# A two-block transformer on one core: first mixer rewritten with a column-tiled convolution and TensorE's order by hand

## The chip, the cores and the metric

One core of one Trainium2 chip runs the whole program. The metric is the device time of one execution in microseconds. Before the change it was 1336.69 us, the median of 3 runs (1336.37 to 1338.35).

Words used below: PE is TensorE, PEld its weight loads, DVE is VectorE, ACT is ScalarE, POOL is GpSimd, SP is the engine from whose queue nearly all DMAs are issued.

## What is computed

256 tokens of width 1024 pass through one block of a first model and two blocks of a second, in float32. Only the first block's mixer is touched:

```
h = rms_norm(x, norm1_g); proj = h @ w_in            # 1024 -> q, k, v (512 each), u (1024)
q, k = rope(rms_norm(q)), rope(rms_norm(k))          # 8 heads of 64, per-head norm
attn = softmax(q k^T / 8, causal) v
a, g = split(u + glu_b); c = a * sigmoid(g)
conv = silu(layer_norm(depthwise_causal_conv31(c) + dw_b))   # 512 channels, 31 taps
x = x + concat(attn, conv) @ w_out
...
x = x + (silu(h @ w_gate) * (h @ w_up)) @ w_down
```

The second model's blocks follow: a feed-forward, a mixer and a feed-forward, twice.

## The kernel before

Tokens are two tiles of 128 (t = 0, 1). Every large product keeps float32 accuracy with three fp32r matmuls of 512 columns: activations and weights are each split into a hi part (ACT copies to fp32r) and a lo part (DVE subtracts), and `mm3` (L270) adds hi*hi, hi*lo and lo*hi in PSUM. Weights are stored as a list of blocks (`plan`, L80) of 128 x 2048 floats, 1 MB each; `load` (L211) issues one DMA per block on SP into three rotating buffers with the tag raw, `split` (L225) makes hi and lo halves of 1024 columns in eight rotating buffers (wh, wl), and `take` (L257) hands blocks to the matmuls and keeps the splits two blocks ahead. A projection (`project`, L467) is two blocks: 48 matmuls for both tiles.

The tile framework's scheduler orders the instructions of each engine by priority; every engine then runs its own list strictly in order, and SP issues its DMAs strictly in order.

The first mixer (`mixer1`, L672) projects a and g (`project2`, L476: tile 0 for both, then tile 1, since tile 1's input arrives later), adds bias, takes the sigmoid, multiplies, transposes the product into four tiles hc of 128 channels x 286 positions (30 zeros ahead), and convolves. The 31 taps of channels 0 to 127 and 128 to 255, and 12 of the third group, are 74 operations on DVE of 128x256 (`conv_dve`, L733), placed in portions between the other work by `bg` (L746). The other 50 taps are fp32 matmuls on PE with a diagonal 128x128 weight each (`conv_pe`, L714), whose diagonals come by DMA, four at a time (tag dg). Queries and keys are normed per head with eight squares each on ACT (L762), rotated on DVE (`rope`, L523) and transposed (`to_T`, L537). Scores, softmax and transposed probabilities follow (`scores`, L602), the v projection, the attention sum (`attend`, L618: two heads side by side in column tiles of 64), the layer norm of the convolution (L792 to L811), and `w_out` (L491), first its attention half, then its convolution half. `ends` (L450) adds to the residual xres and makes the next block's transposed input (`norm_in`, L299).

At the start (`run`, L970) SP loads an identity, x in two pieces for tile 0, constants, the first weight block in four pieces, x for tile 1 and more blocks; `norm_in` transposes x on PE before the first matmul.

Of the kernel before, what the change touches and what calls it, by code (L numbers as in the profile page):

```python
# [14 lines left out]
P = 128  # L15
# [64 lines left out]
def plan():  # L80
# [3 lines left out]
    b += out_blocks("w_out", (0,), (0, 1))  # L84
# [40 lines left out]
C_DWW = 76  # L125
C_SUB = 200
NCOL = 201
# [48 lines left out]
class K:  # L176
    def __init__(self, tc, aps, pools):
        self.tc, self.nc = tc, tc.nc
        self.w, self.x_in, self.cols_in, self.rows_in, self.sh_in, self.rev_in, self.dg_in, self.out = aps
# [31 lines left out]
    def load(self):  # L211
# [7 lines left out]
        q = n // 4 if i == 0 else n // 2 if i == 1 else n  # L219
        for a in range(0, n, q):  # L220
            self.nc.sync.dma_start(r[:, a : a + q], src[:, a : a + q])
# [3 lines left out]
    def split(self):  # L225
# [9 lines left out]
        for a in range(0, n, h):  # L235
            wh = self.hl.tile([P, 2048 // NPART], F32R, tag="wh", name=self.nm("wh"))
            wl = self.hl.tile([P, 2048 // NPART], F32R, tag="wl", name=self.nm("wl"))
            step = min(h, FIRST_SPLIT if i < 2 else SPLIT)
# [60 lines left out]
    def norm_in(self, t, idx):  # L299

        nc = self.nc
        xh = self.xp.tile([P, D], F32R, tag=f"xh{t}", name=self.nm("xh"))
        xl = self.xp.tile([P, D], F32R, tag=f"xl{t}", name=self.nm("xl"))
# [12 lines left out]
        self.xT[t] = (xh, xl)  # L316

    def xlhs(self, t):
        xh, xl = self.xT[t]
# [155 lines left out]

    def project2(self, widths, between=None):  # L476
# [14 lines left out]
    def w_out(self, lhs0, lhs1, post, nxt, mid=None):  # L491

        ps = [[self.mmt(), self.mmt()] for _ in range(2)]
        for h in range(2):
            (b,) = self.take(1)
            for t in range(2):
                self.block_mm(ps[t][h], b, lambda k: lhs0(t, k), 0, True, False)
        bs = self.take(2, 2)
# [50 lines left out]
    def softmax_rows(self, t, qT, kT, heads, mask):  # L549
# [8 lines left out]
        for g in range(0, n, 2 * per):  # L558
# [7 lines left out]
            for h in hs:  # L566
# [7 lines left out]
                es[h] = s  # L574
        return es, sm
# [25 lines left out]

    def scores(self, qT, kT, mask):  # L602

        out = []
        for t in range(2):
            es, sm = self.softmax_rows(t, qT, kT, list(range(8)), mask[t] if isinstance(mask, list) else mask)
            pt = self.probs_T(t, es, list(range(8)))
            rs = self.small(8, "rs")
            self.nc.vector.reciprocal(rs, sm)

            rb, rr = self.slot(), self.slot()
            self.nc.vector.tensor_copy(
                rb[:, :].rearrange("p (h d) -> p h d", d=64), rs[:, :].unsqueeze(2).broadcast_to([P, 8, 64]))
            self.nc.scalar.activation(rr, self.transpose4(rb), AF.Copy)
            out.append((pt, rr))
        return out

    def attend(self, sc, v):  # L618

        nc = self.nc  # L620
        res = []
        for t in range(2):
            pt, rr = sc[t]
            o = self.att()
            for h in range(8):
                r, c = (h % 2) * 64, (h // 2) * P
                for kb in range(t + 1):
                    nc.tensor.matmul(  # L628
                        o[r : r + 64, c : c + P], v[kb][:, h * 64 : (h + 1) * 64], pt[(h, kb)],
                        start=(kb == 0), stop=(kb == t), tile_position=(0, r))  # L630
            on = self.slot()
            nc.vector.tensor_tensor(on, o, rr, op=ALU.mult)
            res.append(self.split_T(on))
        return res
# [37 lines left out]
    def mixer1(self, nxt):  # L672
# [20 lines left out]

        pa, pg = self.project2((512, 512), between=lambda: self.norm_in(1, 0))
        for t in range(2):
            self.norm_rstd(t)
        hc = [self.slot() for _ in range(4)]
        for c in range(4):
            nc.gpsimd.memset(hc[c][:, 0:30], 0.0)
        for t in range(2):  # L700
            r = self.rstd[t][:, 0:1]
            a, g = self.slot(), self.slot()
            nc.vector.scalar_tensor_tensor(a, pa[t], r, glu[:, :512], op0=ALU.mult, op1=ALU.add)
            nc.vector.scalar_tensor_tensor(g, pg[t], r, glu[:, 512:], op0=ALU.mult, op1=ALU.add)
            nc.scalar.activation(g, g, AF.Sigmoid)
            nc.vector.tensor_tensor(a, a, g, op=ALU.mult)
            tp = self.transpose4(a)
# [3 lines left out]
        w = lambda c, k: self.cols[:, C_DWW + c * 31 + k : C_DWW + c * 31 + k + 1]  # L711
        cps = {}

        def conv_pe(c):  # L714
            ks = list(range(CONV_DVE[c], 31))
            if not ks:
                return
            if not cps:
                cps["bank"] = self.mmt()
            ps = cps[c] = cps["bank"][:, (c % 2) * 256 : (c % 2 + 1) * 256]  # L720
            for g in range(0, len(ks), 4):
                dg = self.sl.tile([P, 512], F32, tag="dg", name=self.nm("dg"), bufs=DG_BUFS)
                nk = len(ks[g : g + 4])
                nc.sync.dma_start(
                    dg[:, : nk * P].rearrange("p (k m) -> p k m", k=nk),
                    self.dg_in[c, ks[g] : ks[g] + nk].rearrange("k p m -> p k m"))
# [340 lines left out]
```

## Time and profile before

| | |
|---|---|
| median of the runs | 1336.69 us |
| the profiled execution, its own time | 1337.39 us |
| its span, first to last instruction | 1335.6 us |
| PE busy | 1308.6 us, 98% |
| DVE busy | 794.9 us, 60% |
| ACT busy | 682.7 us, 51% |
| start of the third projection | 36.06 us |
| first matmul of the first feed-forward | 142.08 us |

Times in the rows count from the span's start. A timeline row merges neighbours of one kind: its second number is the time from the first one's start to the last one's end, and matmuls overlap, so that the spacing of starts, not the length, is what one costs. A plain fp32 matmul leaves two records.

### The profile page before, as it was taken

What the parts mean: (1) busy time and instruction counts of PE and PEld (TensorE: products, weight loads), DVE (VectorE), ACT (ScalarE), POOL (GpSimd) and SP (SyncE); (2) the same over time, 40 slices, a digit from 0 to 9 for tenths busy, and PEclk for the clock granted to TensorE, in tenths of its full rate; (3) what the DMA queues carried; (4) which work ended last, traced back from release to release, by engine and by line L of the source; (5) the groups of instructions that cost most, each with busy time, mean ns of one, the idle gap of its engine ahead of it and who ended that gap; (6) DMA issues with size and microseconds to landing.
All of it is one profiled execution on the core that took longest, in us unless ns stands there. A gap on an engine that the chain in (4) does not pass through costs nothing.

```text
span 1335.6 us, 16190 instructions
## 1 busy us (share of the span) xinstructions
PE 1308.6 (98%) x6226; PEld 1065.8 (80%) x6226; DVE 794.9 (60%) x1249; ACT 682.7 (51%) x1131; POOL 33.4 (3%) x47
## 2 busy tenths in 40 slices
PE   7989999999999999999999999999999999999998
PEld 5767888888888888777888888888888777888886
DVE  5888655545555547897665544755546554755543
ACT  5663644435545435756654444654435856744431
POOL 0100000000000000000000000000000000000000
PEclk9999999999999999999999999999999999999999
DMA  8652465554655554533365555555554452465540
GB/s 297 218 193 85 163 211 189 189 175 157 219 178 189 185 177 157 193 127 115 126 246 191 172 181 183 207 187 189 189 189 170 161 188 99 172 219 185 187 164 32
DMA packets 43470, 235.55 MB, mean 176 GB/s; under 512 B 4864, under 2 KB 13696, under 8 KB 16640
## 3 DMA queue, kind: packets, MB, share of 16 engines
q1 hardware_dynamic: 43392, 234.51, 50.7%
q8 instruction: 49, 0.80, 0.2%
q14 instruction: 29, 0.24, 0.1%
HBM read 233.44 MB, written 1.05 MB: 176 GB/s over the span
## 4 chain that ended last, share of the span: by engine, by line
PE 90%; DVE 4%; ACT 2%; DMA 1%; POOL 1%; issue 1%; SPq 0%; POOLq 0%; DVEq 0%; ACTq 0%
PE mm L272 27%; PE mm L274 27%; PE mm L273 27%; PE tp L382 2%; PE at L565 1%; DVE wl L243 1%; PE tp L308 1%; DMA dg<-dg 1%; PE mm L729 1%; PE tp L520 1%; PE tp L586 1%; PE at L628 1%; DVE slot L741 1%; DMA raw<-w 1%; POOL qf L285 1%
## 5 line engine op out<-in xcount | busy, mean ns | idle before, releaser
L243 DVE TENSOR_TENSOR wl<-raw,wh 128x1024 fp32r<-128x1024 f32 (+2 forms) x430 | 514.3, 1208 | 409.5 <-ACT wh L242 396.4
L242 ACT ACTIVATE wh<-raw 128x1024 fp32r<-128x1024 f32 (+2 forms) x430 | 444.0, 1049 | 500.9 <-PE mm L274 472.9
L272 PE MATMUL mm<-wh,xh 128*128 128x512 f32 (+1 forms) x1168 | 458.5, 393 | 2.5 <-ACT wh L242 2.5
L273 PE MATMUL mm<-wl,xh 128*128 128x512 f32 (+1 forms) x1168 | 456.2, 391 | 0.6 <-DVE wl L243 0.6
L274 PE MATMUL mm<-wh,xl 128*128 128x512 f32 (+1 forms) x1168 | 456.5, 391 | 0.0
L272 PEld LDWEIGHTS mm<-wh,xh 128*128 128x128 f32 x1168 | 219.9, 188 | 48.4 <-ACT wh L242 3.8
L273 PEld LDWEIGHTS mm<-wl,xh 128*128 128x128 f32 x1168 | 219.7, 188 | 46.6 <-DVE wl L243 2.4
L274 PEld LDWEIGHTS mm<-wh,xl 128*128 128x128 f32 x1168 | 219.9, 188 | 44.5 <-issue 0.2
L272 PE MATMUL mm<-wh,slot 128*128 128x512 f32 x536 | 211.0, 394 | 0.0
L274 PE MATMUL mm<-wh,slot 128*128 128x512 f32 x536 | 209.8, 392 | 0.0
L273 PE MATMUL mm<-wl,slot 128*128 128x512 f32 x536 | 209.7, 391 | 0.0
L272 PEld LDWEIGHTS mm<-wh,slot 128*128 128x128 f32 x536 | 100.7, 188 | 21.5 <-issue 1.5
L274 PEld LDWEIGHTS mm<-wh,slot 128*128 128x128 f32 x536 | 100.6, 188 | 20.7
L273 PEld LDWEIGHTS mm<-wl,slot 128*128 128x128 f32 x536 | 100.7, 188 | 20.0
L313 ACT ACTIVATE xh<-tp,cols 128x128 fp32r<-128x128 f32 x128 | 42.5, 369 | 30.4 <-PE tp L308 16.6
L424 DVE SCALAR_TENSOR_TENSOR slot<-mm,rstd,slot 128x512 f32<-128x512 f32 (+1 forms) x60 | 41.7, 702 | 18.3 <-PE mm L274 18.3
L314 DVE SCALAR_TENSOR_TENSOR xl<-tp,cols,xh 128x128 fp32r<-128x128 f32 x128 | 40.6, 346 | 20.0 <-ACT xh L313 19.0
L572 ACT ACTIVATE e<-e,mx 128x128 f32<-128x128 f32 (+1 forms) x80 | 35.4, 446 | 7.6 <-DVE mx L569 7.6
L423 ACT ACTIVATE slot<-mm,rstd 128x512 f32<-128x512 f32 (+1 forms) x60 | 36.5, 658 | 3.6 <-PE mm L274 3.4
L385 DVE TENSOR_TENSOR slot<-tp,slot 128x512 fp32r<-128x512 f32 (+1 forms) x60 | 35.9, 639 | 0.0
L337 ACT ACTIVATE junk<-mm 128x512 bf16<-128x512 f32 x24 | 14.4, 600 | 36.6 <-PE mm L274 36.6
L741 DVE SCALAR_TENSOR_TENSOR slot<-slot,cols,slot 128x256 f32<-128x256 f32 x71 | 32.2, 479 | 0.5
(117 smaller groups left out, 652.8 us busy)
## 6 DMA issues: line engine op xcount, KB each, us to landing
raw<-w SPq DMA_DIRECT2D x209, 1024.0 KB, 4.9
gb<-rows SPq DMA_DIRECT2D x7, 512.0 KB, 5.5
dg<-dg SPq DMA_DIRECT2D x11, 256.0 KB, 2.9
bias<-rev SPq DMA_DIRECT2D x2, 1024.0 KB, 7.4
raw<-w SPq DMA_DIRECT2D x2, 592.0 KB, 3.8
raw<-w SPq DMA_DIRECT2D x4, 256.0 KB, 6.1
raw<-w SPq DMA_DIRECT2D x2, 512.0 KB, 8.4
out<-xres SPq DMA_DIRECT2D x4, 256.0 KB, 2.0
```

Of the source, the lines that this page charges most:

```text
L242: self.nc.scalar.activation(wh[:, o], r[:, i_], AF.Copy)
L243: self.nc.vector.tensor_tensor(wl[:, o], r[:, i_], wh[:, o].bitcast(F32), op=ALU.subtract)
L272: mm(ps, xh, wh, start=start, stop=False)
L273: mm(ps, xh, wl, start=False, stop=False)
L274: mm(ps, xl, wh, start=False, stop=stop)
L313: nc.scalar.activation(xh[:, c], tp[:, j * P : (j + 1) * P], AF.Copy, scale=g)
L314: nc.vector.scalar_tensor_tensor(xl[:, c], tp[:, j * P : (j + 1) * P], g, xh[:, c].bitcast(F32), op0=ALU.mult, op1=ALU.subtract)
L385: nc.vector.tensor_tensor(hlo[:, :cw], tp, hh[:, :cw].bitcast(F32), op=ALU.subtract)
L423: nc.scalar.activation(sg[:, :cw], pg[t], AF.Silu, scale=r)
L424: nc.vector.scalar_tensor_tensor(sg[:, :cw], pu[t], r, sg[:, :cw], op0=ALU.mult, op1=ALU.mult)
L572: nc.scalar.activation(s[:, :nk], s[:, :nk], AF.Exp, bias=mx[:, h : h + 1], scale=-1.0, accum_out=sm[:, h : h + 1])
L741: nc.vector.scalar_tensor_tensor(a, hc[c][:, k : k + 256], w(c, k), a, op0=ALU.mult, op1=ALU.add)
```

## The change

What it does, part by part:

- **Start.** Eight matmuls of zeros stand first on PE. x (transposed on the host) and the first two weight blocks come packed together in four pieces (`first`), the first of them in two DMAs; no transposes on PE for the first input. All eight k-slices are split straight from these pieces (`start`).
- **Order.** Inside `mixer1_body` PE runs in the order in which the code is written (`manual_schedule`); other engines are still scheduled. Transposes and small matmuls stand at chosen places between the projections' matmuls (`project_with`, `w_out`'s `between`).
- **Convolution.** All on PE. For each of four channel groups, four 32-channel quarters are column tiles of 32; a matmul's 128 rows are 32 channels times four shifts of the input by 8, so that 8 matmuls per quarter cover the 32 taps (the last is zero). The shifted input xc is made by 16 DMAs per group from hc, 64 in all, issued as soon as hc is whole (`conv_load`); the weights cw come in two DMAs of 1 MB into raw buffers.
- **Norm of q and k.** One square of 512 columns on ACT and a reduction on DVE, in place of eight squares with accumulated sums.
- **w_out** takes the convolution's half first; its end, with the next block's transposes, lies in the hand-written order too.
- Small tiles elsewhere change their tags; behind the first feed-forward block the order of every engine is as before.

```diff
-FIRST_SPLIT = 512
-DG_BUFS = 2
-CONV_DVE = (31, 31, 12, 0)
-BG = (10, 10, 24, 20)
+XC_BUFS = 3
+WARM = 8
+CG = 8
+CW = CG + 255
...
-    b += out_blocks("w_out", (0,), (0, 1))
+    b += out_blocks("w_out", (0,), (1, 0))
...
+    def start(self):
+        nc = self.nc
+        nc.scalar.dma_start(self.cols[:, C_G : C_G + 8], self.cols_in[:, C_G : C_G + 8])
+        self.x_halves(0)
+        xh, xl = [a[:, :].rearrange("p (t c) -> p t c", t=2) for a in self.xT]
+        parts = []
+        for p in range(4):
+            r = (self.raw if p < 3 else self.gp).tile(
+                [P, 2048], F32, tag="raw" if p < 3 else "bias", name=self.nm("first"))
+            for a, n in ((0, 768), (768, 768)) if p == 0 else ((0, 1536),):
+                nc.sync.dma_start(r[:, a : a + n], self.first_in[p][:, a : a + n])
...
+                nc.scalar.activation(wh[:, o], u, AF.Copy)
+                nc.scalar.activation(xh[:, :, c], x, AF.Copy, scale=g)
+                nc.vector.tensor_tensor(wl[:, o], u, wh[:, o].bitcast(F32), op=ALU.subtract)
...
+    def project_with(self, between, ncols=512, nb=2):
+        ps = [self.mmt(ncols), self.mmt(ncols)]
+        n = 0
+        for i in range(nb):
+            (b,) = self.take(1)
+            nk = b[1][3]
+            for k in range(nk):
+                if n in between:
+                    between[n]()
+                for t in range(2):
+                    self.mm3(
+                        ps[t], *self.xlhs(t)(b[1][2] + k), *self.part(b, k * ncols, ncols),
+                        i == 0 and k == 0, i == nb - 1 and k == nk - 1)
+                n += 1
+        return ps
...
-        pa, pg = self.project2((512, 512), between=lambda: self.norm_in(1, 0))
         for t in range(2):
             self.norm_rstd(t)
+        with self.tc.manual_schedule(engines={PE}):
+            self.mixer1_body(glu, tabs, nxt)
...
+        def glu_T(t):
+            tp = self.transpose4(ag[t])
+            for c in range(4):
+                nc.scalar.activation(hc[c][:, 30 + t * P : 30 + (t + 1) * P], tp[:, c * P : (c + 1) * P], AF.Copy)
+            if t == 1:
+                conv_load()
...
+        def conv_load():
+            for c in range(4):
...
+                for s in range(4):
+                    for i in range(4):
+                        nc.sync.dma_start(
+                            xc[32 * s : 32 * s + 32, i * CW : (i + 1) * CW],
+                            hc[c][32 * i : 32 * i + 32, 8 * s : 8 * s + CW])
...
+        def conv(c):
+            if c % 2 == 0:
+                cps["w"] = self.raw.tile([P, 2048], F32, tag="raw", name=self.nm("cw"))
+                nc.sync.dma_start(cps["w"], self.cw_in[c // 2])
+                cps["bank"] = self.mmt()
...
+            for g in range(CG):
+                for i in range(4):
+                    o = ((c % 2) * 4 + i) * 32 * CG + g * 32
+                    nc.tensor.matmul(
+                        ps[32 * i : 32 * i + 32, :], wt[:, o : o + 32], xc[:, i * CW + g : i * CW + g + 256],
+                        start=(g == 0), stop=(g == CG - 1), tile_position=(0, 32 * i))
...
-                for h in range(8):
-                    c = slice(h * 64, (h + 1) * 64)
-                    nc.scalar.activation(sq[:, c], ps[t][:, c], AF.Square, accum_out=ss[:, h : h + 1])
+                nc.scalar.activation(sq, ps[t], AF.Square)
+                nc.vector.tensor_reduce(ss, sq[:, :].rearrange("p (h d) -> p h d", d=64), axis=AX.X, op=ALU.add)
...
+        pq = self.project_with({3: lambda: glu_T(0), 5: lambda: glu_T(1)})
+        qT, kT = [self.slot(), self.slot()], [self.slot(), self.slot()]
+        q = qk_norm(pq, 0)
+        pk = self.project_with({5: lambda: self.to_T(q[0], qT, 0), 7: lambda: self.to_T(q[1], qT, 1)})
+        k = qk_norm(pk, 1)
+        conv(0)
+        conv(1)
+        self.to_T(k[0], kT, 0)
...
+        st[0][0]()
+        conv(2)
+        self.to_T(k[1], kT, 1)
+        st[1][0]()
+        conv(3)
+        pt = [self.probs_T(0, sm[0][0], heads), {}]
+        st[1][1]()
...
+        pv = self.project_with({
+            1: lambda: ln_a(0), 3: lambda: (probs(heads[:4]), inv(0)), 4: lambda: ln_a(1),
+            6: lambda: (probs(heads[4:]), inv(1)), 7: lambda: ln_b(0)})
+        v = self.vcopy(pv)
+        ln_b(1)
...
+        self.w_out(part(cv, 4), part(att, 0), None, nxt, {
+            2: lambda: att.append(self.attend_t(0, (pt[0], rr[0]), v)),
+            3: lambda: att.append(self.attend_t(1, (pt[1], rr[1]), v))})
...
+        for _ in range(WARM):
+            nc.tensor.matmul(ps[:, :P], z[:, :P], z[:, :P], start=True, stop=True)
+        self.start()
+        self.load()
```

`st` holds the three groups of scores and softmax (tile 0; tile 1, heads 0 to 3 and 4 to 7). In the lists below xc is the shifted input, slot_340 to slot_343 are hc, cw is the convolution's weight.

SP's queue behind the loads of the k and v projections, before the change (raw is a weight block, dg four diagonals):

```order
L221 DMA raw_222<-w 128x2048
L724 DMA dg_942<-dg 128x4x128
L221 DMA raw_395<-w 128x2048
L724 DMA dg_948<-dg 128x4x128
L221 DMA raw_413<-w 128x2048
L221 DMA raw_447<-w 128x2048
L221 DMA raw_559<-w 128x2048
L354 DMA gb_2722<-rows 128x1024
L943 DMA bias_8262<-rev 128x8x256
L221 DMA raw_593<-w 128x2048
L221 DMA raw_869<-w 128x2048
L221 DMA raw_903<-w 128x2048
```

and with it:

```order
L220 DMA raw_366<-w 128x2048
L220 DMA raw_409<-w 128x2048
L802 DMA xc_434<-slot_340 32x263 x16
L802 DMA xc_451<-slot_341 32x263 x16
L802 DMA xc_468<-slot_342 32x263 x16
L802 DMA xc_485<-slot_343 32x263 x16
L220 DMA raw_564<-w 128x2048
L220 DMA raw_598<-w 128x2048
L810 DMA cw_684<-cw 128x2048
L810 DMA cw_798<-cw 128x2048
L220 DMA raw_938<-w 128x2048
```

The 64 copies now stand together, ahead of the two next weight blocks and of cw; before, single loads of diagonals stood between the blocks.

PE between the k projection and the scores, with the change (mm_686 is the convolution's bank, slot_658 is k of tile 0, at the scores):

```order
L271 MATMUL mm_563<-wh_415,xh_102 128x512
L272 MATMUL mm_563<-wl_416,xh_102 128x512
L273 MATMUL mm_563<-wh_415,xl_103 128x512
L816 MATMUL mm_686<-xc_434,cw_684 32x256 x32
L816 MATMUL mm_686<-xc_451,cw_684 32x256 x32
L575 MATMUL tp_753<-sh,slot_658 128x128 x4
L621 MATMUL at_764<-slot_522,slot_520 128x128
```

Before, tap matmuls stood in fours and less between transposes and scores, behind the v projection:

```order
L729 MATMUL mm_941<-slot_344,dg_942 128x256 x4
L520 MATMUL tp_686<-sh,slot_679 128x128 x4
L586 MATMUL tp_729<-sh,e_705 128x128
L729 MATMUL mm_941<-slot_344,dg_948 128x256
L586 MATMUL tp_729<-sh,e_708 128x128
L586 MATMUL tp_729<-sh,e_711 128x128
L565 MATMUL at_756<-slot_627,slot_481 128x256
L565 MATMUL at_757<-slot_627,slot_481 128x256
L586 MATMUL tp_729<-sh,e_714 128x128
```

Two groups of convolution, 32 matmuls each, now stand in one piece ahead of k's transposes, the scores and the v projection.

DVE at the gate, before (L703 and L704 add the bias, L706 multiplies, L243 is a lo split):

```order
L243 TENSOR_TENSOR wl_398<-raw_177,wh_397 128x1024
L704 SCALAR_TENSOR_TENSOR slot_350<-mm_224,rstd_332,gb_132 128x512
L703 SCALAR_TENSOR_TENSOR slot_364<-mm_277,rstd_339,gb_132 128x512
L243 TENSOR_TENSOR wl_402<-raw_177,wh_401 128x1024
L706 TENSOR_TENSOR slot_349<-slot_349,slot_350 128x512
L704 SCALAR_TENSOR_TENSOR slot_365<-mm_302,rstd_339,gb_132 128x512
L243 TENSOR_TENSOR wl_406<-raw_187,wh_405 128x1024
L706 TENSOR_TENSOR slot_364<-slot_364,slot_365 128x512
```

and with the change (L778 and L780 for L704 and L706, L242 for L243; wl_275 is the first lo half of the third projection):

```order
L778 SCALAR_TENSOR_TENSOR slot_356<-mm_271,rstd_192,gb_161 128x512
L780 TENSOR_TENSOR slot_266<-slot_266,slot_352 128x512
L780 TENSOR_TENSOR slot_268<-slot_268,slot_356 128x512
L242 TENSOR_TENSOR wl_275<-raw_198,wh_274 128x1024
L242 TENSOR_TENSOR wl_279<-raw_198,wh_278 128x1024
L242 TENSOR_TENSOR wl_309<-raw_232,wh_308 128x1024
L242 TENSOR_TENSOR wl_313<-raw_232,wh_312 128x1024
```

The first lo half of the third projection stood ahead of the gate, and now stands behind the whole of it.

## Rows read from the trace of the kernel before

**Rows 1.** The page: engines' busy time (1) and the chain that ended last, by engine (4).

```profile
PE 1308.6 (98%) x6226; PEld 1065.8 (80%) x6226; DVE 794.9 (60%) x1249; ACT 682.7 (51%) x1131; POOL 33.4 (3%) x47
...
PE 90%; DVE 4%; ACT 2%; DMA 1%; POOL 1%; issue 1%; SPq 0%; POOLq 0%; DVEq 0%; ACTq 0%
```

**Rows 2.** Table of windows, whole core: stretch, length, busy time of each engine, clock, DMA.

```profile
0.00:8.33 8.33, 2.20 (x9) 1.44 (x9) 0.88 (x4) 2.70 (x5) 0.30 (x5) 1.00 0.62 176
8.33:36.06 27.73, 26.20 (x105) 19.84 (x106) 20.34 (x44) 19.54 (x35) 1.35 (x6) 1.00 0.83 306
36.06:142.08 106.02, 97.11 (x506) 76.70 (x504) 88.38 (x196) 58.92 (x174) 8.86 (x8) 1.00 0.49 164
142.08:1335.60 1193.52, 1183.13 (x5611) 967.81 (x5609) 685.31 (x1007) 601.54 (x920) 22.92 (x28) 1.00 0.50 174
```

**Rows 3.** Timeline of PE: first matmuls, four transposes, steady matmuls; start, length, line, form, count.

```profile
8.33 0.80 PE L272 MATMUL mm<-wh,xh 128*128 128x512 f32 x1 [1.59 <-ACT wh L242]
...
13.00 0.43 PE L272 MATMUL mm<-wh,xh 128*128 128x512 f32 x1
...
39.03 0.60 PE L520 MATMUL tp<-sh,slot 128*128 128x128 f32 x4
...
150.06 0.39 PE L272 MATMUL mm<-wh,xh 128*128 128x512 f32 x1
...
158.90 0.39 PE L272 MATMUL mm<-wh,xh 128*128 128x512 f32 x1
```

**Rows 4.** Timeline of PE: scores (L565), old convolution (L729), attention in two column tiles (L628).

```profile
72.82 1.16 PE L565 MATMUL at<-slot,slot 64*128 64x128 f32 x16
...
85.20 1.14 PE L565 MATMUL at<-slot,slot 64*128 64x256 f32 x8
...
95.49 3.80 PE L729 MATMUL mm<-slot,dg 128*128 128x256 f32 x16 [1.63 <-DMA dg<-dg]
99.22 1.96 PE L628 MATMUL at<-slot,slot 128*64 128x128 f32 x28
```

**Rows 5.** DVE's groups by line and form, 0 to 142 us: busy us, mean ns.

```profile
L243 DVE TENSOR_TENSOR wl<-raw,wh 128x1024 fp32r<-128x1024 f32 x30 | 36.2, 1219 | 2.8 <-ACT wh L242 2.1 <-DMA slot<-rows 0.6
L741 DVE SCALAR_TENSOR_TENSOR slot<-slot,cols,slot 128x256 f32<-128x256 f32 x71 | 32.2, 479 | 0.5
...
L533 DVE TENSOR_TENSOR slot<-mm,slot 128x256 f32<-128x256 f32 x4 | 1.7, 418 | 0.0
...
L704 DVE SCALAR_TENSOR_TENSOR slot<-mm,rstd,gb 128x512 f32<-128x512 f32 x2 | 1.5, 751 | 3.5 <-PE mm L274 3.5
...
L706 DVE TENSOR_TENSOR slot<-slot,slot 128x512 f32<-128x512 f32 x2 | 1.4, 685 | 0.0
```

**Rows 6.** The same, ACT.

```profile
L242 ACT ACTIVATE wh<-raw 128x1024 fp32r<-128x1024 f32 x31 | 32.0, 1071 | 11.6 <-DMA raw<-w 7.1 <-PE mm L274 4.5
...
L808 ACT ACTIVATE slot<-tp,cols 128x128 f32<-128x128 f32 x8 | 3.0, 454 | 0.0
...
L709 ACT ACTIVATE slot<-tp 128x128 f32<-128x128 f32 x8 | 1.6, 294 | 0.0
...
L808 ACT ACT_TABLE_LOAD x1 | 1.3, 1283 | 0.0
L705 ACT ACTIVATE slot<-slot 128x512 f32<-128x512 f32 x2 | 1.3, 632 | 3.9 <-DVE slot L704 3.9
```

**Rows 7.** Timeline of SP: start, length and count of DMA issues.

```profile
2.58 1.86 SPq L221 DMA_DIRECT2D raw<-w  x4
...
9.11 0.33 SPq L354 DMA_DIRECT2D gb<-rows  x1
...
35.81 0.43 SPq L724 DMA_DIRECT2D dg<-dg  x1
```

**Rows 8.** DMA, 0 to 150 us: GB/s by slices of 3.75 us; issue to landing, us.

```profile
GB/s 123 220 341 427 337 152 433 304 310 55 321 354 374 302 214 151 133 85 194 33 247 70 256 85 292 272 283 27 144 78 117 0 0 55 225 203 81 0 210 227
...
raw<-w SPq DMA_DIRECT2D x19, 1024.0 KB, 5.0
```

More of the change, by code (lines that the diff above doesn't have):

```diff
@@ L557, in softmax_rows, with group @@
         sm = self.small(8, "sm")
-        for g in range(0, n, 2 * per):
+        def group(g):
             hs = heads[g : g + 2 * per]
@@ L574, in softmax_rows @@
                 es[h] = s
+        if parts is not None:
+            parts += [lambda g=g: group(g) for g in range(0, n, 2 * per)]
+        else:
+            for g in range(0, n, 2 * per):
+                group(g)
         return es, sm
@@ L607, in scores, with attend_t @@
             pt = self.probs_T(t, es, list(range(8)))
[L608 to L615, printed above, removed]
-        return out
-    def attend(self, sc, v):
[L620 to L624, printed above, removed]
-            for h in range(8):
[L626 to L634, printed above, removed]
+            out.append((pt, self.inv_rows(sm)))
+        return out
+    def attend_t(self, t, sc, v):
+        nc = self.nc
+        pt, rr = sc
+        o = self.att()
+        for h in range(8):
+            r, c = (h % 2) * 64, (h // 2) * P
+            for kb in range(t + 1):
+                nc.tensor.matmul(
+                    o[r : r + 64, c : c + P], v[kb][:, h * 64 : (h + 1) * 64], pt[(h, kb)],
+                    start=(kb == 0), stop=(kb == t), tile_position=(0, r))
+        on = self.slot()
+        nc.vector.tensor_tensor(on, o, rr, op=ALU.mult)
+        return self.split_T(on)
+    def attend(self, sc, v):
+        return [self.attend_t(t, sc[t], v) for t in range(2)]
     def scaled_tables(self, t, co, si, w, mul):
@@ L692, in mixer1, with mixer1_body @@
             tabs.append(a)
-        pa, pg = self.project2((512, 512), between=lambda: self.norm_in(1, 0))
         for t in range(2):
             self.norm_rstd(t)
+        with self.tc.manual_schedule(engines={PE}):
+            self.mixer1_body(glu, tabs, nxt)
+    def mixer1_body(self, glu, tabs, nxt):
+        nc = self.nc
+        pa = self.project()
+        ag = []
+        for t in range(2):
+            a = self.slot()
+            nc.vector.scalar_tensor_tensor(a, pa[t], self.rstd[t][:, 0:1], glu[:, :512], op0=ALU.mult, op1=ALU.add)
+            ag.append(a)
+        pg = self.project()
         hc = [self.slot() for _ in range(4)]
@@ L712, in mixer1 @@
         cps = {}
[L714 to L718, printed above, removed]
-                cps["bank"] = self.mmt()
[L720 to L726, printed above, removed]
-                for j, k in enumerate(ks[g : g + 4]):
-                    d = dg[:, j * P : (j + 1) * P]
-                    nc.tensor.matmul(ps, d, hc[c][:, k : k + 256], start=(k == ks[0]), stop=(k == 30))
@@ L744, in mixer1 @@
-        it = conv_dve()
-        def bg(n):
-            for _ in range(n):
-                next(it, None)
-        ops = []
-        for which in range(2):
-            bg(BG[which])
-            ps = self.project()
-            dst = [self.slot(), self.slot()]
+        acc = [self.slot()[:, :256] for _ in range(4)]
+        def conv_load():
+            for c in range(4):
+                if c == 0:
+                    xc = self.gp.tile([P, 2048], F32, tag="bias", name=self.nm("xc"))
+                else:
+                    xc = self.gp.tile([P, 4 * CW], F32, tag="xc", name=self.nm("xc"), bufs=XC_BUFS)
+                for s in range(4):
[3 more added lines that the diff above has]
+                            hc[c][32 * i : 32 * i + 32, 8 * s : 8 * s + CW])
+                xcs.append(xc)
@@ L756, in mixer1, with qk_norm @@
+        def qk_norm(ps, which):
+            res = []
             for t in range(2):
@@ L1020, in build @@
         ):
-            K(tc, (w, x, cols, rows, sh, rev, dg, out), (cp, raw, hl, sl0, xp, gp, sm, psm, pst)).run()
+            K(tc, (w, x, first, cols, rows, sh, rev, cw, out), (cp, raw, hl, sl0, xp, gp, sm, psm, pst)).run()
 def kernel(**inputs):
```

167 lines of the change are left out of this document (93 added, 74 removed).

## The prediction

> **What bounds the kernel now.** I read the page first: TensorE is busy 98% of the span and the chain that ended last runs through it for 90% [rows 1]. So only what TensorE has to do, or waits for, counts. The table of windows then says where the change can act [rows 2]: it touches the time up to 142.08 us, where the feed-forward's first matmul starts; the order of every engine behind that is the same in both programs, and there PE is busy 1183.1 of 1193.5 us. In the first 142.08 us it is busy 125.5. The rest is 16.6 us of idle time, and 22.8 us of the busy time is the convolution, so a rewritten mixer has something to win. Time is the profiled execution's (1337.4 us, span 1335.6); the median of the runs is 0.7 below it.
>
> Prices used throughout. A 512-column matmul takes 0.227 us (39 starts in 8.84 us) [rows 3]. A transpose takes 0.1 us: four take 0.60 us, of which the last one's own length is 0.28 [rows 3]. A plain fp32 matmul of 256 columns makes two records of (3.80 - 0.39) / 15 = 0.228 us each [rows 4]; the 50 of the old convolution cost 100 x 0.228 = 22.8. A split of a weight half-block is 1.22 us on DVE and 1.07 on ACT [rows 5, 6]. SP needs, back to back, (1.86 - 0.43) / 3 = 0.475 us to issue one DMA of 128 rows (four quarter blocks in one row); one that SP had to wait for took 0.33, and one of 512 pieces, right behind another, no more than 0.43 [rows 7].
>
> **Step 1, the start: 7 us won.** PE now starts at 8.33 and the third projection at 36.06 [rows 2]. The packed loads bring the first 0.39 MB first. With the rates of the old start (slices of 3.75 us: 0.46 MB by 3.75 us, 1.29 by 7.5, 2.57 by 11.25, 4.17 by 15) [rows 8] it lands near 3.3 us and all 3.15 MB by 12.6. ACT and DVE then spend about 1.1 us on each of eight k, the last is ready at 15.0, the first projection ends at 18.4, and the second 48 x 0.227 = 10.9 later, at 29.3. That removes 16 transposes (1.6) and most of the waits. The zero matmuls matter little: the first ten matmuls took 4.67 us instead of 2.27 (0.43 apart near 13 us, so 1.2 GHz of the two levels) [rows 3], but in the new order PE waits for the loads in that stretch anyway; 0 to 1 us.
>
> **Step 2, the gate: 3.8 us given back.** On DVE the gated products now stand ahead of the first split for the third projection. Behind the last matmul come 0.75 (bias add), 0.63 (sigmoid), 1.07 (hi part on ACT, the product of 0.69 on DVE beside it), 1.22 (lo part) and 0.1 of matmul tail [rows 5, 6]: 3.8 us until PE's second matmul. Third projection: 33.1 to 44.8.
>
> **Step 3, the copies: the step that decides.** The copies of the convolution's input are 64 DMAs of 32 partitions on SP, and they need the second transposed half: 30 matmuls into the third projection (6.8), transposes, and ACT's copies of 0.29 [rows 6] behind two hi splits. SP can begin at 41.3. 64 x 0.475 = 30.4 us: the last is issued at 71.7. Only then come two weight blocks and the convolution's own weights, cw. A 1 MB load lands 5.0 us after its issue [rows 8]; the third of three, at 2.4 us each at the row's 433 GB/s, 9.8 after the first's issue. cw lands at **81.5**. PE has been ready since about 60: 44.8, 10.9 of matmuls, 0.8 of transposes, and some 3.8 of waits for q, whose two norms share DVE with four splits: five passes of 512 and two of 256 columns, 3.6 us a norm at 0.69 and 0.42 [rows 5], so 2 x 3.6 + 4 x 1.22 = 12.1 us behind the third projection. That is 21 us of idle TensorE, before the first of the convolution's matmuls. I take 0.475 because the 64 stand back to back, as the row's four do. The bounds: 0.38 (0.33 and the gap of 0.05) gives 6.2 less; below, a share of 32 rows in 128 of it (0.12) is the first rival.
>
> **Step 4, from the convolution to the feed-forward: 73.5 us.** Work of PE: convolution 256 records x 0.228 = 58.4 us, four column tiles abreast 14.6; I take 15. The one row with column tiles has 28 records of 128 columns in 1.96 us, 0.062 each against 0.107 alone: two tiles run nearly side by side [rows 4]; at that yield four would need 17. The Trainium skill (TensorE: Matmul & The Clock Gate, section "Measured speedup vs the span model") measured 3.07 times for four row tiles and 2.38 for three column tiles. By it the convolution would take 19 us and the sum would be 4 higher; no run of this kernel shows four tiles. Then 56 transposes (5.6), scores (1.16 + 2 x 1.14 = 3.4), attention 48 x 0.062 = 3.0, and 144 matmuls of 512 columns (32.6): 59.6 us. Waits that the hand order cannot fill, 13.9: low clock after the long pause, 2.4 (as at the start); k's copies behind the convolution's eviction, 1.1; the second scores behind a table load of 1.28 and eight exponentials, 2.0; in the v projection the inverse sums and the layer norm, which stand behind splits of 1.22 on DVE, 3.0; ahead of w_out a table load, four silu pieces (0.45 each), a split and the hi part (1.28 + 1.8 + 1.07 + 0.6 less 1.85 under the last matmuls of v) [rows 6], 2.9; at its end, where the next block's transposes now stand behind all of w_out, 2.5. What the change takes off DVE (71 tap operations of 0.48 us and three first ones) [rows 5] and off ACT (32 squares become 4) sets nothing here: both engines stand idle while PE waits for cw.
>
> **Sum.** 81.5 + 73.5 = 155.0, against 142.1: **+12.9**. 1337.4 + 12.9 - 0.7 = **1349.6 us**. Its own range, with 0.38 a copy and 4 us fewer waits below, 17 for the convolution and 6 more of waits above, is 1339 to 1358.
>
> **Rivals.** *Copies of 32 rows are cheap to issue* (the other side). For: each has a quarter of the rows of every DMA in the trace. Against: 512 pieces cost no more than 128. At 0.12 us the copies are out by 49, and cw waits for its buffer instead, which the last k split frees at 57.7; it lands at 62.7. Without the pause's low clock 71.1 follow: 133.8, 8.3 less than now, 1328.4 (1326 to 1334). The point: PE must start the convolution by 142.1 - 73.5 = 68.6, so (68.6 - 41.3 - 9.8) / 64 = 0.27 us a copy; above that the change loses.
>
> *The column tiles run two abreast only.* For: no row has more than two. Against: those two do run side by side. 128 x 0.228 = 29.2, 14.2 more: 1364.
>
> *Level.* Copies at 0.33 and half of the 13.9 waits: 81.5 - 9.3 - 7 + 73.5 = 138.7, 3.4 less than now; with 0.38 a copy 141.8. 1333 to 1337.
>
> *Part of it does nothing*: if the zero matmuls do not lift the clock, step 1 loses up to 1 us; it changes no sign.
>
> **Chances.** Forecast 0.57, cheap copies 0.27, two abreast 0.09, level 0.07. 0.2% (2.7 us) is about what a measurement of this kernel tells from no change. Faster: cheap copies and a little of level, 0.29; within 0.2%: 0.06; slower: 0.65. The range 1328 to 1358 leaves out the two-abreast case and the lower end of the cheap one, some 0.2.
>
> **What would show it.** In the changed profile: SP's row of 64 copies 30 us long, cw's issue behind it near 73; PE's wait before the convolution's first matmul some 20 us, put down to the DMA of cw; 256 convolution records in 14 to 19 us; matmuls 0.43 apart behind the pause; the feed-forward's first matmul near 155. Step 1 is right if the third projection starts at 33; step 2 if its second matmul waits 3 to 4 us for a DVE split. The forecast is wrong if the copies are issued under 0.27 us apart, or if PE reaches the convolution with cw in place.

## The result, and the profile with the change

| | before | with the change |
|---|---|---|
| median of the runs | 1337.4 us | 1368.72 us |
| span of the profiled execution | 1335.6 us | 1366.8 us |
| first feed-forward's first matmul | 142.08 us | 171.76 us |

The kernel before was run again beside it (1337.4 in these runs, 1336.69 in the first three). The ratio is 1.0234, 95% interval 1.0216 to 1.0252: slower by 31 us, where 13 were forecast. The direction was right, and the size was off by more than the range (1339 to 1358) allowed.

The page of the changed kernel, engines' busy time and the chain that ended last, beside [rows 1]:

```profile
PE 1305.8 (96%) x6382; PEld 1062.9 (78%) x6382; DVE 767.2 (56%) x1171; ACT 680.7 (50%) x1067; POOL 33.9 (2%) x51
...
PE 90%; SPq 3%; DVE 2%; ACT 2%; DMA 1%; issue 1%; POOL 0%; POOLq 0%; DVEq 0%; ACTq 0%
```

TensorE has 2.8 us less to do than before and DVE 28 less, and yet the span is 31 longer. What is new is SP's queue in the chain, with 3% of the span. The table of windows cuts the start at the third projection (32.78), the end of the k projection (62.50), the first convolution matmul (96.15), the v projection (119.92), w_out (141.67) and the feed-forward (171.76); the columns are those of [rows 2]:

```profile
0.00:32.78 32.78, 27.24 (x112) 21.41 (x113) 18.88 (x41) 18.97 (x31) 1.79 (x15) 1.00 0.81 322
32.78:62.50 29.72, 25.98 (x112) 20.49 (x112) 21.05 (x30) 14.76 (x26) 3.29 (x2) 0.94 0.42 143
62.50:96.15 33.65, 0.23 (x2) 0.03 (x1) 11.02 (x20) 4.79 (x6) 3.58 (x2) 0.55 0.39 133
96.15:119.92 23.77, 22.26 (x305) 16.61 (x305) 4.25 (x26) 10.88 (x35) 0.52 (x1) 0.92 0.57 203
119.92:141.67 21.75, 16.45 (x91) 13.07 (x89) 10.44 (x26) 13.14 (x26) 1.12 (x2) 0.99 0.25 95
141.67:171.76 30.09, 29.44 (x153) 23.19 (x153) 15.09 (x19) 14.15 (x21) 0.55 (x1) 0.90 0.32 107
171.76:1366.80 1195.04, 1184.17 (x5614) 968.08 (x5614) 686.47 (x1013) 604.05 (x926) 23.03 (x28) 1.00 0.50 174
```

In the third row PE stands still for nearly all of the 33.65 us: it is busy 0.23 of them, DVE 11.0 and ACT 4.8. The last row says that 1.5 us more lie behind the feed-forward's start than before (1195.0 against 1193.5 [rows 2]). Three views name the reason of the stop. SP's timeline:

```profile
43.83 41.96 SPq L802 DMA_DIRECT2D xc<-slot  x64
85.89 1.00 SPq L220 DMA_DIRECT2D raw<-w  x2
86.99 7.83 SPq L810 DMA_DIRECT2D cw<-cw  x2
```

PE's timeline there (L816 is the convolution, 64 records a group; idle time ahead of a row, and what ended it, in brackets):

```profile
96.15 5.72 PE L816 MATMUL mm<-xc,cw 128*32 128x256 f32 x64 [33.42 <-DMA cw<-cw]
102.44 3.85 PE L816 MATMUL mm<-xc,cw 128*32 128x256 f32 x64 [0.56 <-ACT slot L819]
...
108.44 3.67 PE L816 MATMUL mm<-xc,cw 128*32 128x256 f32 x64
```

and the page's DMA issues, median us to landing:

```profile
xc<-slot SPq DMA_DIRECT2D x64, 32.9 KB, 1.9
cw<-cw SPq DMA_DIRECT2D x2, 1024.0 KB, 6.9
```

A copy lands 1.9 us after its issue, so the moving of the data is quick. But SP stands 42 us over the 64 issues, only then come the v weights, and only then cw, for which PE waits 33.4 us. This is the mechanism that was forecast, and larger: PE's stop is 33.4 us where some 21 were forecast, and cw is there at 96.15 where 81.5 was.

### The profile page after: what moved, and what is told of

It is laid out like the page before. It is cut to its first block, busy times and chain, and to the rows that moved or that the text cites. A ratio compares the mean times of both kernels' runs of the same rounds, so it can differ in the third digit from the quotient of the medians.

```text
span 1366.8 us, 16443 instructions
## 1 busy us (share of the span) xinstructions
PE 1305.8 (96%) x6382; PEld 1062.9 (78%) x6382; DVE 767.2 (56%) x1171; ACT 680.7 (50%) x1067; POOL 33.9 (2%) x51
## 4 chain that ended last, share of the span: by engine, by line
PE 90%; SPq 3%; DVE 2%; ACT 2%; DMA 1%; issue 1%; POOL 0%; POOLq 0%; DVEq 0%; ACTq 0%
PE mm L273 27%; PE mm L272 27%; PE mm L271 27%; SPq L802 3%; PE tp L414 2%; PE mm L816 1%; PE at L621 1%; PE tp L575 1%; PE tp L306 1%; PE at L690 1%; PE tp L648 1%; DVE wl L242 1%; DMA cw<-cw 1%; DMA first<-first 0%; PE at L964 0%
## 5 line engine op out<-in xcount | busy, mean ns | idle before, releaser
L242 DVE TENSOR_TENSOR wl<-raw,wh 128x1024 fp32r<-128x1024 f32 (+1 forms) x422 | 508.5, 1219 | 442.2 <-ACT wh L241 429.4
L241 ACT ACTIVATE wh<-raw 128x1024 fp32r<-128x1024 f32 (+1 forms) x422 | 439.5, 1058 | 525.3 <-PE mm L273 475.8
L273 PEld LDWEIGHTS mm<-wh,slot 128*128 128x128 f32 x536 | 101.2, 189 | 21.8 <-DVE slot L565 0.8
L311 ACT ACTIVATE xh<-tp,cols 128x128 fp32r<-128x128 f32 x112 | 37.4, 371 | 25.0 <-PE tp L306 14.7
L816 PE MATMUL mm<-xc,cw 128*32 128x256 f32 x256 | 16.9, 415 | 34.0 <-DMA cw<-cw 33.4
L312 DVE SCALAR_TENSOR_TENSOR xl<-tp,cols,xh 128x128 fp32r<-128x128 f32 x112 | 35.6, 347 | 15.4 <-ACT xh L311 14.1
L816 PEld LDWEIGHTS mm<-xc,cw 128*32 128x32 f32 x256 | 12.6, 119 | 37.7 <-ACT wh L241 33.8
L628 ACT ACTIVATE e<-e,mx 128x128 f32<-128x128 f32 (+1 forms) x80 | 35.4, 447 | 6.9 <-DVE mx L625 6.9
## 6 DMA issues: line engine op xcount, KB each, us to landing
xc<-slot SPq DMA_DIRECT2D x64, 32.9 KB, 1.9
```

What stands on the lines that cost most here:

```text
L241: self.nc.scalar.activation(wh[:, o], r[:, i_], AF.Copy)
L242: self.nc.vector.tensor_tensor(wl[:, o], r[:, i_], wh[:, o].bitcast(F32), op=ALU.subtract)
L273: mm(ps, xl, wh, start=False, stop=stop)
L311: nc.scalar.activation(xh[:, c], tp[:, j * P : (j + 1) * P], AF.Copy, scale=g)
L312: nc.vector.scalar_tensor_tensor(xl[:, c], tp[:, j * P : (j + 1) * P], g, xh[:, c].bitcast(F32), op0=ALU.mult, op1=ALU.subtract)
L816: nc.tensor.matmul(ps[32 * i : 32 * i + 32, :], wt[:, o : o + 32], xc[:, i * CW + g : i * CW + g + 256], start=(g == 0), stop=(g == CG - 1 ...
```

## Experiments

The theory after the result: SP's issues of the copies, each 0.63 us, and what stands behind them in its queue are the whole loss. The main rivals are that the copied input itself comes late whatever the order, and that the new order and convolution are no better than the old ones even without the wait.

### The weights ahead of the copies

```diff
+            cw_load()                 # first half of cw, ahead of all copies
             for c in range(4):
+                if c == 1:
+                    cw_load()         # second half
```

> The 64 copies stay; the convolution's weights move ahead of them on SP (first block ahead of all copies, second behind the first group's 16). Theory (the 64 issues of 0.63 us on SP and what stands behind them are the whole loss): the convolution starts at about 62.5 us instead of 96.2, then waits only for its own groups, the last of which lands at about 87; the v weights, still behind the copies, land near 93, so the v projection starts near 95 instead of 120 and the feed-forward near 147 instead of 171.8: some 1342 us. Rival (the copied input itself comes late, or the copies collide with the loads): the convolution starts no earlier than 85, over 1355 us.

Measured: 1349.81 us, ratio to the kernel before 1.0091 (1.0074 to 1.0107), so 19 us of the 31 came back. The convolution starts at 62.60. PE's waits in the mixer have a new row (us in total, times, longest):

```profile
PE mm L824 <- DMA xc<-slot: 5.6, 3, 3.7
```

and SP's timeline has the v weights behind the copies:

```profile
89.23 5.23 SPq L220 DMA_DIRECT2D raw<-w  x3
```

Now PE waits for the input's groups, three times and together 5.6 us. The rival that the input is late whatever the order, with a start no earlier than 85, falls. But the copies now set the pace: PE's weight loads (PEld) wait for them within the groups too,

```profile
PEld mm L824 <- DMA xc<-slot: 4.2, 9, 0.5
```

and three of the four groups of 64 records take 5.5 to 6.9 us instead of 3.7. With the v projection, whose weights are issued from 89 on and which starts at 96.1 and lasts 28.7 us instead of 21.8, this puts the time 8 us above the expectation.

### Three of four copies left out

```diff
-                    for i in range(4):
+                    for i in (s,):
```

> 48 of the 64 copies are left out (one of four per shift stays; the rest of the shifted input is zeros set on POOL), so the convolution computes on zeros there. Theory: SP is through its 16 copies at 54, cw lands near 63, PE waits about 1 us, and without the low clock behind the pause the feed-forward starts at 136 to 138: 1331 to 1334 us. Rival (the hand order and its waits cost as much as the new start and convolution win): the feed-forward starts at 142 or later, 1337 us or more.

Measured, one execution: 1336.09 us. The convolution, which computes on zeros for the most part, starts at 63.78, but the feed-forward at 139.09, later than the theory's 136 to 138 and earlier than the rival's 142. From the convolution to the feed-forward it takes 75.3 us, so this stretch is longer than I had put it. By this one execution, what is left of the change beside 48 of the copies is about level with the kernel before.

### What an issue costs, by its form

```diff
-                        nc.sync.dma_start(xc[32 * s : ...], hc[c][32 * i : ...])
+                        # by group: 32 rows of 1052 or 1024 bytes, 128, 64, 16 rows from hc;
+                        # 32 and 128 rows from cw in memory
+                        nc.sync.dma_start(dst, a)
```

> 64 DMAs in the copies' place, of several forms: 16 as they are (32 rows of 1052 bytes, on-chip to on-chip), 8 of 32 rows of 1024 bytes, 8 of 128 rows of 1052 bytes on-chip, 8 of 32 rows from memory, 8 of 128 rows from memory, 8 of 64 and 8 of 16 rows on-chip. The convolution's input is then not the shifted one. If few rows make an issue dear: 0.59 for both kinds of 32 rows, 0.43 for 128 rows, more for 16. If on-chip to on-chip makes it dear: 0.59 for all on-chip forms, 0.43 from memory. If the row length of 1052 bytes makes it dear: 0.43 for 1024 bytes alone.

SP's timeline, cut at places where one form stands alone: in this order 32 rows of 1052 bytes, 32 of 1024, 128 rows, 64 rows and 16 rows, all from on-chip memory to on-chip memory; then 32 rows and 128 rows from the chip's main memory to on-chip memory:

```profile
43.68 2.49 SPq L821 DMA_DIRECT2D xc<-slot  x4
...
54.60 4.32 SPq L821 DMA_DIRECT2D xc<-slot  x7
...
63.48 2.40 SPq L821 DMA_DIRECT2D xc<-slot  x4
...
75.99 1.87 SPq L821 DMA_DIRECT2D xc<-slot  x3
...
81.82 3.74 SPq L821 DMA_DIRECT2D xc<-slot  x6
...
68.25 0.95 SPq L821 DMA_DIRECT2D xc<-cw  x2
...
73.42 0.80 SPq L821 DMA_DIRECT2D xc<-cw  x2
```

On-chip to on-chip an issue takes 0.62, 0.62, 0.60, 0.62 and 0.62 us (a row's length over its count; the starts stand some 0.63 apart), with 16 rows as with 128; from memory 0.475 and 0.40, by two issues each. The number of rows and the row's length do nothing. An on-chip source alone does not make an issue dear either: the stores from the chip to memory, of the runs below, are no dearer than loads (four in 1.8 us). What is dear is a copy with both its ends on the chip. By two more rows the price shows in the length of the next issue: a load from memory right behind on-chip copies takes 0.58 us, an on-chip copy right behind loads 0.49:

```profile
59.60 0.58 SPq L821 DMA_DIRECT2D xc<-cw  x1
...
69.31 0.49 SPq L821 DMA_DIRECT2D xc<-slot  x1
```

### The same 64 transfers, read from memory

```diff
+                nc.sync.dma_start(hd[c], hc[c][:, : CW + 24])
...
-                            hc[c][32 * i : 32 * i + 32, 8 * s : 8 * s + CW])
+                            hd[c][32 * i : 32 * i + 32, 8 * s : 8 * s + CW])
```

(hd is a buffer in the chip's main memory.)

> The changed kernel with its 64 transfers of 32x263 left as they are in number, size and place on SP, but read from memory, where four stores of 128x287 put the input first. Theory (an on-chip source makes an issue 0.63 us, a source in memory 0.475, as the prediction's price was): SP needs 30.4 us for them and is through near 78 instead of 86, cw lands near 88, the feed-forward starts at 163 to 165: some 1358 us. Rival (0.63 us is the price of small transfers of any source): 1370 us or more, the stores on top.

Measured: 1355.93 us, 1.0133 (1.0118 to 1.0149). SP's timeline has the 64 issues:

```profile
46.68 32.89 SPq L806 DMA_DIRECT2D xc<-hd  x64
```

and PE's the start of the convolution:

```profile
87.42 5.25 PE L820 MATMUL mm<-xc,cw 128*32 128x256 f32 x64 [24.22 <-DMA cw<-cw]
```

The row is 9.1 us shorter (32.9 against 42.0), and the convolution starts 8.7 us earlier, though four stores and their landing were put ahead. Of each row 28 issues stand without a pause, first of the change, then of this run:

```profile
43.83 17.70 SPq L802 DMA_DIRECT2D xc<-slot  x28
```

```profile
52.93 12.93 SPq L806 DMA_DIRECT2D xc<-hd  x28
```

That is 0.63 us an issue against 0.46, with the same number, size and target. Near the price that the prediction used (0.51 us with the pauses in the row), the change loses 18 us, stores and all.

### Sixteen loads in place of 64 copies

```diff
+                nc.sync.dma_start(hd[c], hc[c][:, : CW + 24])
...
-                    for i in range(4):
-                        nc.sync.dma_start(xc[...], hc[c][...])
+                    nc.sync.dma_start(
+                        xc[32 * s : 32 * s + 32, : 4 * CW].rearrange("p (i w) -> p i w", i=4),
+                        hd[c][:, 8 * s : 8 * s + CW].rearrange("(i p) w -> p i w", p=32))
```

> The same input through memory: 4 stores of 128x287 and 16 loads of 32x4x263 in place of the 64 copies, all else as in the change. Theory: 20 issues of some 0.45 us, the input is whole near 58, cw lands near 63, the feed-forward starts at 136 to 139: 1331 to 1335 us. Rival (the round trip through memory, or loads of 32 rows, are as slow as the copies): the convolution starts after 75, over 1345 us.

Measured: 1338.69 us, 1.0009 (0.9999 to 1.0018). SP's timeline:

```profile
43.19 1.79 SPq L803 DMA_DIRECT2D hd<-slot  x4
...
46.88 11.78 SPq L805 DMA_DIRECT2D xc<-hd  x16
...
59.34 3.44 SPq L813 DMA_DIRECT2D cw<-cw  x2
```

and PE's longest wait in the mixer:

```profile
PE mm L819 <- DMA cw<-cw: 6.2, 1, 6.2
```

The 30 us are back, by fewer issues and a source in memory. cw still stands last and lands at 68.

### Both repairs

Two of the edits together: the weights ahead, and sixteen loads in place of the copies.

> Both repairs: the input through memory (4 stores, 16 loads) and the convolution's weights ahead of it on SP. Theory: the convolution's weights land near 50 and the input near 60, so the convolution starts at 62 to 63 instead of 68.2 (memory alone) and 67.0 (weights first alone); with no pause before it the clock stays at its higher level, 64 records in 3.7 us instead of 5.6. The feed-forward starts at 133 to 135: 1329 to 1332 us, 5 to 8 less than before. Rival (a next wait of the same size stands behind this one, the v weights or the second scores): 1336 or more.

Measured: 1335.61 us, 0.9985 (0.9976 to 0.9994). The convolution starts at 61.94, as expected, and runs 64 records in 3.67 to 3.85 us. But the feed-forward starts at 138.34, not at 134: the time lies nearer to the rival's (1336 or more) than to the theory's (1329 to 1332), as a next wait stood behind. The v projection took 26.8 us (83.71 to 110.55) instead of 20.7 with the sixteen loads alone. DVE's timeline there:

```profile
91.34 0.29 DVE L726 TENSOR_TENSOR slot<-slot 128x128 f32<-128x128 f32 x1 [3.06 <-DMA slot<-rows]
91.55 0.80 DVE L890 TENSOR_SCALAR slot<-tp,bmv,brv 128x512 f32<-128x512 f32 x1
```

and the longest of PE's waits:

```profile
PE tp L649 <- DVE slot L890: 3.5, 1, 3.5
```

L726 belongs to a constant of the second model. Its row load stands on SP behind weight blocks that wait for buffers, is issued at 82.80 and lands 8.5 us later; DVE waits for it, and the layer norm (L890), for which PE waits, is behind it. The 6.1 us are more than the wait itself, as the clock is at its lower level behind PE's stop, where it was 1.00 through the v projection of the sixteen loads alone:

```profile
92.50:99.92 7.42, 6.26 (x22) 5.09 (x23) 2.73 (x6) 2.84 (x5) 0.00 (x0) 0.54 0.65 234
```

### The zero matmuls

`WARM = 0`, in the kernel with both repairs.

> As the run with both repairs, without the eight zero matmuls. Theory: PE waits for the first loads in that stretch anyway, so the third projection starts within 1 us of where it does with them: 0 to 1 us more. Rival (they lift the clock in time for the first real matmuls): 2 to 4 us more.

Measured: 1336.23 us, 0.9993 (0.9984 to 1.0002), 0.6 above the run with them, the intervals overlapping. The expectation of 0 to 1 us holds, though no difference can be told from none.

### Half the copies from POOL's queue

```diff
-                        nc.sync.dma_start(
+                        (nc.sync if c < 2 else nc.gpsimd).dma_start(
```

> The changed kernel with the 32 copies of groups 2 and 3 issued from POOL's queue, all else as it is. Theory: SP is through at 64 instead of 86, cw lands near 75, and as POOL does little else its 32 copies are out in time if one takes it under 0.9 us: the feed-forward starts near 150 instead of 171.8, some 1345 us. Rival (POOL's issues are dearer than SP's, over 1.5 us each): the last group comes after 93 and the convolution waits in its middle, 1355 us or more.

Measured: 1351.96 us, 1.0101 (1.0085 to 1.0116). SP's half, in its timeline:

```profile
46.27 20.25 SPq L802 DMA_DIRECT2D xc<-slot  x32
```

POOL's:

```profile
58.56 12.39 POOL L802 DMA_DIRECT2D xc<-slot  x25
78.77 3.27 POOL L284 TENSOR_TENSOR qf<-qms,mhalf 128x8 f32<-128x8 f32 x2
```

and PE's wait:

```profile
PE mm L816 <- DMA cw<-cw: 14.8, 1, 14.8
```

Halving SP's row moved the convolution from 96.2 to 80.0. POOL takes 0.50 us a copy, less than SP, so the rival of dearer issues there falls. The start is 5 us behind the expected landing of cw (75), as SP began 2.4 us later in this run and cw landed 9.7 us (median) after its issue; the time is 7 us above the expectation. And POOL's small power operation for the norm of k (L284) stood behind its copies until 78.8: here a queue's issues cost the engine's own work its turn, though PE was waiting for cw until 80.0 anyway.

### Four small moves on top of both repairs

The six small loads for q's and k's norms behind the third projection's weights; then also the constant of the second model behind the mixer; then also the spreading of the inverse sums right behind the sums; and last the second half of cw behind all loads of the input:

```diff
-        tabs = [...]                       # six row loads, ahead of the first projection
+        tabs = [...]                       # behind the gate
-        self.lambda_()                     # ahead of the v projection
+        self.lambda_()                     # behind w_out
-            rr[t] = self.inv_rows(sm[t][1])
+            nc.scalar.activation(rr[t], self.transpose4(rbs[t]), AF.Copy)   # rbs made behind the sums
-                if c == 1:
-                    cw_load()
+            cw_load()                      # behind the loop
```

> As the run with both repairs, and the six small loads of the norms' gains, which SP issues one by one with a wait of 1.3 us each ahead of the third projection's weights, go behind those weights; the tables made from them go behind the gate. Theory: the third projection's weights are loaded 8 us earlier and the first of them split while ACT and DVE wait for the second projection, so PE's pause of 2.45 us before the third projection falls to below 1 and the matmuls behind it stay 0.23 apart: 2 to 4 us less than the run with both repairs. Rival (the gate's additions and sigmoid set the pause, not the weights): no difference.

> As the run with both repairs and the later tables, and the 128x256 row load with its five small operations, which only the second model needs, goes behind the first mixer. In the run with both repairs DVE stood 3.1 us in the v projection waiting for that load, with the layer norm behind it in its queue. Theory: the v projection up to w_out takes 21 us, as where that load came in time, instead of 25 to 27: 3 to 5 us less, 1330 to 1332 us. Rival (the second v block or the splits set it): within 1 us of the run before.

> As the run before, and the two copies that spread the softmax's inverse sums over 512 columns stand on DVE right behind their sums instead of behind splits in the v projection. Theory: PE's two waits of together 2.3 us for these copies go: 1 to 2.5 us less. Rival (PE then waits for the next thing in the same place, the layer norm or the transposed probabilities on ACT): within 0.5 us.

> As the best run so far (1332.4 us), and the convolution's second block of weights goes behind all of the input's loads on SP instead of between the first group's and the second's, where SP waited for its buffer until 58 us. Theory: the second group's input is there when the first group is done, so PE's wait of 3.1 us between them goes, with the second block landing near 66, ahead of the third group: 2 to 3 us less, 1330 us. Rival (the second block now comes late for the third group, at 74): no difference.

Measured, ratio to the kernel before: 0.9982 (0.9971 to 0.9993), 0.9982 (0.9973 to 0.9991), 0.9958 (0.9946 to 0.9971) and 0.9949 (0.9935 to 0.9962); medians 1334.99, 1335.65, 1332.4 and 1330.89 us. The first is a miss: PE's stop ahead of the third projection fell from 2.45 and 0.76 to 1.75 us in one piece, and the time by no more than the intervals can tell. The second shows its mechanism and not its gain: the v projection took 21.8 us instead of 25.2, but the convolution started 1.6 later in that profile (64.05 against 62.43), and the ratio is the same. The third came as expected in the v projection (both waits gone, 19.8 us instead of 21.8), and its time is 3 us lower; but in its profile the convolution also started 3.4 us earlier (60.70) and a new wait of 3.1 for the input's second group came, so how much of the 3 the two waits are is not shown. The fourth removed that wait of 3.1 us, but another of 1.9 for ACT's copies of k came, the feed-forward starts 0.7 later in its profile (134.63 against 133.96), and the intervals of the two overlap. Together the last kernel is 6.6 us faster than the kernel before (1330.89 against 1337.52), and 38 faster than the change as it was made. Its table of windows from the third projection on, cut at the same places as above:

```profile
31.35:61.52 30.17, 25.30 (x111) 19.91 (x111) 22.20 (x39) 13.62 (x25) 3.29 (x2) 0.95 0.70 224
61.52:86.58 25.06, 22.05 (x306) 12.62 (x305) 15.07 (x46) 15.00 (x40) 4.10 (x3) 0.92 0.86 279
86.58:105.26 18.68, 16.31 (x91) 13.09 (x89) 9.48 (x22) 12.94 (x25) 1.11 (x2) 1.00 0.35 125
105.26:134.63 29.37, 28.23 (x152) 22.44 (x152) 15.54 (x22) 15.60 (x23) 0.55 (x1) 0.94 0.35 115
```

The stage of 33.65 us without work is gone, and the feed-forward starts at 134.63.

## Why the prediction was wrong

**The step that failed is step 3, by the price of an issue.** "I take 0.475 because the 64 stand back to back, as the row's four do" took a row of loads from memory for copies within the chip. Measured: 0.63 us, which the experiment on forms puts down to a source and a target that are both on the chip. Between the forecast of 155.0 and the measured 171.76, and behind it, the 18.3 us that were missing go to:

| term | forecast | measured | more |
|---|---|---|---|
| first copy issued | 41.3 | 43.83 | 2.5 |
| 64 issues | 30.4 | 41.96 | 11.6 |
| last copy to cw's landing | 9.8 | 10.4 | 0.6 |
| convolution to feed-forward | 73.5 | 75.6 | 2.1 |
| behind the feed-forward's start | 0 | 1.5 | 1.5 |

Of the 11.6, 64 x (0.633 - 0.475) = 10.1 are the price, the rest are short waits among them. The bounds were the second fault: 0.38 and 0.475 came from loads, and the text looked only below for another price (0.12, a share by rows). No DMA of before goes from the chip to the chip; a bound above should have been kept, as nothing excluded one.

The last term, behind the feed-forward's start, was put at nothing on the ground that the order behind 142.08 is the same in both programs. The change leaves it the same only behind the first feed-forward block. Near that block's start PE now has eight transposes (first row), where it had four in the kernel before (second row):

```profile
176.40 1.04 PE L306 MATMUL tp<-sh,xres 128*128 128x128 f32 x8
```

```profile
144.36 0.60 PE L308 MATMUL tp<-sh,xres 128*128 128x128 f32 x4
```

Counted from the feed-forward's first matmul, its twentieth of 512 columns comes 1.2 us later than before, and the lag stays near that.

**Step 1 was near**: the second projection ends at 30.33 (forecast 29.3), and the zero matmuls, worth 0.6 us by medians whose intervals overlap, fit the forecast of 0 to 1. **Step 2 was right**: from the end of the second projection (30.33) to the third projection's second matmul (34.04, forecast 33.1) it takes 3.7 us (forecast 3.8), most of them PE's waits for the hi part and, last, for the split on DVE:

```profile
32.78 0.50 PE L271 MATMUL mm<-wh,xh 128*128 128x512 f32 x1 [2.45 <-ACT wh L241]
34.04 0.50 PE L272 MATMUL mm<-wl,xh 128*128 128x512 f32 x1 [0.76 <-DVE wl L242]
```

What it did not foresee is the clock after it: between 34.5 and 39 us the granted clock is 0.62, matmuls stand 0.43 apart, and eight of them so (35.33 to 38.73) cost 1.6 of the 2.5 us by which the copies started late; the other 0.9 came with the second matmul. A slip in step 3's account of q, five passes of 0.69 and two of 0.42, which are 4.3 us and not 3.6, does not enter the sum.

**Step 4 was near, its rivals less so.** Four column tiles do run abreast: 64 records in 3.67 us are 0.057 each against 0.228, so a quarter, and the rival of two abreast falls. The convolution took 16.9 us (5.72 + 3.85 + 2 x 3.67) for the forecast 15, as its first group ran at the lower level behind the stop (granted clock 0.50 from 96.15 to 100.18). By the 3.07 times that the Trainium skill (TensorE: Matmul & The Clock Gate, section "Measured speedup vs the span model") has for four row tiles it would be 19, an estimate; the trace's factor is 4.0 at full clock, not 2.38 or 3.07. That the stretch came out only 2.1 us over its forecast is in part luck. By the table of windows PE's waits in it are 7.5 us (1.5 + 5.3 + 0.65), where 11.5 stood beside the low clock's 2.4; and the clock fell a second time, at the start of w_out, where ten matmuls stand 0.43 apart (0.90 over that window), which the forecast does not have.

**The rival of cheap copies was too good.** With input and weights in time it gave 1328.4; the run with both repairs has 1335.6. Its 71.1 us from the convolution to the feed-forward were 76.4 there, where a wait moved up: the constant's row load, behind which DVE stood, and the low clock behind it. Where that load was in time the stretch is near the forecast: 72.0 with the sixteen loads alone (68.24 to 140.26), 72.3 with the load moved away (64.05 to 136.32). The break-even point came out: with the input through memory the convolution starts at 68.24, within 0.4 us of the point that was named (68.6), and the ratio is 1.0009, level. But starting it 6 us earlier won only 3.

**Level** has the number of the run without three of four copies (1336.09, inside its 1333 to 1337), but not by its own path: it had the convolution start at 72.2 and 66.5 us behind it, and the run has 63.78 and 75.3.

## What to carry to other kernels

Count the issues that a change puts in front of the next load, not the bytes: 2.1 MB of copies landed in 1.9 us each and still held the queue for 42 us. Take the price of an issue from a row with the same source and the same target, and where none exists, leave the range open above. And once a long wait is repaired, look for the next thing that stands in the same in-order queue: a load that nobody needs yet held DVE, and through it TensorE, for 3 us in the trace, though moving it away did not by itself change the measured time.

## What was not expected of the hardware

- The issue of a DMA from SP takes 0.60 to 0.62 us when its source and its target are both on the chip, with 16, 32, 64 or 128 rows, and 0.40 to 0.475 when it reads from memory; a store from the chip to memory takes 0.45. POOL's queue takes 0.50 for the same on-chip copy.
- Four column tiles of 32 give the full factor of four: 0.057 us a record of 256 columns against 0.228 alone.
- The same stop of 2.45 us ahead of the third projection has a lower clock behind it in one kernel and none in another. The window from 34.5 to 39 us, with the change and then with both repairs:

```profile
34.50:39.00 4.50, 4.50 (x15) 3.48 (x14) 4.50 (x5) 2.98 (x4) 0.00 (x0) 0.62 0.63 208
```

```profile
34.50:39.00 4.50, 4.50 (x24) 3.70 (x23) 4.50 (x5) 3.29 (x7) 0.00 (x0) 1.00 0.73 251
```

The same matmuls stood ahead of it in both, so the length of the stop alone does not tell whether the clock falls; what decides it these runs do not show.
